# A Mamba-2 mixer whose output is kept channel-major instead of token-major

## The chip, the core and the metric

The kernel runs on one core of a Trainium2 chip. The metric is the time of one execution in microseconds of device time; three runs of the kernel before the change gave 2559.63, 2559.95 and 2562.32 us, so the median is 2559.95 us. Every other time below is from one profiled execution of the same kernel.

The engines' names in the profile are PE (TensorE, products), PEld (TensorE's loading of the stationary operand, which overlaps PE), DVE (VectorE), ACT (ScalarE), POOL (GpSimd) and SP (SyncE, here the queue that starts the weights' DMAs).

## The reference

The model is a decoder trunk for 256 tokens of 2048 channels: a Mamba-2 mixer, a gated feed-forward, an attention layer and another gated feed-forward, each followed by a layer norm. Only the mixer is touched. Cut to what matters:

```
zxbcdt = x @ w_in
z   = zxbcdt[..., :4096]
xbc = silu(causal_dwconv(zxbcdt[..., 4096:10240], conv_w, conv_b))
dt  = softplus(zxbcdt[..., 10240:] + dt_bias)
xs, b, c = xbc split in 4096 channels, 8 groups x 128, 8 groups x 128
a  = -exp(a_log)
y  = ssd_chunked(xs * dt, a * dt, b, c)
y  = y + d_skip * xs
y  = y * silu(z)
yg = y in 8 groups of 512 channels
yg = yg * rsqrt(mean(yg ** 2) + RMS_EPS)
y  = yg * norm_w
return y @ w_out
```

`ssd_chunked` works in two chunks of 128 tokens and in 64 heads of 64 channels (eight heads make a group). With `a_cum` the running sum of `a * dt` inside a chunk, it is

```
decay_in     = exp(a_cum[l] - a_cum[s])            where s <= l, else 0
y_diag[l]    = sum over s of (c[l] . b[s]) * decay_in[l, s] * x[s]
state        = sum over s of b[s] * exp(a_cum[end] - a_cum[s]) * x[s]      (first chunk)
y_off[l]     = exp(a_cum[l]) * (c[l] . state)                              (second chunk)
```

## The kernel before

**Weights and steps.** All weights come as one sequence of 512 KB tiles, one per step. A tile is fetched on SP's queue (`load`, L162), and split into two rounded parts `hi` (ScalarE, L183) and `lo` (VectorE, L184) by `split`; activations are kept as such pairs too, and a product of two pairs is made of three products of parts. `splits` (L188) is called in the middle of a step and makes the split of the step three ahead (`LA = 3`), provided that TensorE has freed the buffer. Sixteen rows of 128 input channels and 512 output channels (a chunk) take eight steps.

**Two modes.** In mode "X" (`half`, L196) a tile of the activations, 128 channels by 128 tokens, is the stationary operand and 512 columns of weights stream past it: twelve products 512 wide in a step, and the result is token-major, 128 tokens on the partitions. In mode "W" (`whole`, L225) a 128x128 tile of weights is the stationary operand and the activations stream: eight products of 512 columns (`hi` with both parts of the activations, L243) and eight of 256 (`lo`, L245) in a step, and the result is channel-major. Odd steps of this mode begin with `lo`, even ones with `hi`. A result of mode "W" lies in PSUM in two halves which `gather` (L545) adds: a copy by ScalarE, then a sum by VectorE.

**The order of the rest.** The order of all instructions is the order in which the program writes them: each engine runs its own list in that order and waits where data are missing. `at(i, f)` (L296) puts a function's instructions behind the products of step i. A group g of the mixer takes sixteen steps from `s0 = chX[g].first`: eight for x (mode "W"), eight for z (mode "X"). Its own work stretches over 30 steps, so the first steps of group g+1 (s0+16 is its first) hold the last work of group g; functions of group g that are put at the same step stand ahead of those of g+1.

**A group's work before the change**, by steps from s0 (L774 to L796):

- s0+3 `m_load`: `a_cum` of eight heads broadcast to all partitions by two DMAs on POOL's queue, tiles A[0] and A[1]. POOL waits for the y_diag of the group before, which reads the same buffers.
- s0+6 `m_cb`: the products of C and B in PSUM (L672, L673), masked by VectorE into `cb`; a copy `bc` of the cross-chunk product by ScalarE (L679).
- s0+6 to s0+8 `m_decay`, `m_exp`: A minus `a_cum` of the token on the partition, capped at 0 (VectorE), then the exponential (ScalarE, with a load of its table). At s0+13 and s0+14 `m_mask` multiplies by `cb`.
- s0+4 to s0+9: gather and four taps of the causal convolution of x (`Conv`, L555; the scaled first tap on ScalarE, L572, three taps on VectorE, L577). s0+12 `x_silu`.
- s0+15 `x_turn`: eight transposes of x to token-major (L707), copied to `xs` by ScalarE. s0+16 `x_dt`: VectorE makes `xdt` (x times dt), `xe` (times the decay to the chunk's end) and x times D in `xs`.
- s0+16 `z_silu`: silu of z out of PSUM.
- s0+18 `y_off` and `y_diag` of the first chunk, s0+19 `y_diag` of the second: for each head a product with A as the stationary tile and 64 columns of `xdt` streaming (L723); the sums go into `xs`.
- s0+21 `z_gate`: times silu(z) on VectorE; squares on ScalarE with their sum over the 512 channels, which lie along the free axis.
- s0+22 `z_rms`: mean plus epsilon (VectorE), power -0.5 (POOL). s0+23 `z_scale`: each token's row times its factor.
- s0+28, s0+29 `z_turn`: four transposes each (L340) back to channel-major, then `norm_w` and the split into the two parts of `yT` (ScalarE, VectorE).

After the last group the chunks of `w_out` read `yT` (mode "X").

Of the kernel before, what the change touches and what calls it, by code (L numbers as in the profile page):

```python
# [24 lines left out]
P = 128  # L25
# [20 lines left out]
for _name, _n in (("cw", 4 * CONV), ("cb", CONV), ("nw", DI), ("fw0", 6 * DFF), ("fcb0", 2 * DFF), ("fw1", 6 * DFF),  # L46
                  ("fcb1", 2 * DFF), ("dtb", P), ("alog", P), ("d", NH * P)):
    COL_AT[_name] = N_COL
    N_COL += _n // P
# [9 lines left out]
def chunks():  # L59
# [14 lines left out]
    for g in range(NG):  # L74
        out += some("W", "mamba_w_in", 0, DI + g * NC, 1, KD) + some("X", "mamba_w_in", 0, z + g * NC, 1, KD)
# [15 lines left out]
def yoco_kernel(ctx: ExitStack, tc: tile.TileContext, x, lmg, lmb, lfg, lfb, x_t, columns, w, out):  # L91
# [449 lines left out]
    d_bc = cols[:, COL_AT["d"]:COL_AT["d"] + NH]  # L541
    acum_d = dram.tile([NH, S], F32, name="acum_d")
    aux = mp.tile([P, 6, NH], F32, name="aux")
# [86 lines left out]
    def dt_cum():  # L630

        u, e, q, r, dt, ac, ex = T["t"]
        nc.vector.tensor_scalar(q, dt, T["an"], None, op0=OP.mult)
        nc.vector.memset(r, 1.0)
        for c in range(2):
            sl = slice(c * P, (c + 1) * P)
            nc.vector.tensor_tensor_scan(ac[:, sl], r[:, sl], q[:, sl], 0.0, op0=OP.mult, op1=OP.add)
        nc.gpsimd.dma_start(acum_d, ac)
        nc.scalar.activation(ex[:, :P], ac[:, :P], AF.Exp, bias=ac[:, P - 1:P], scale=-1.0)
        nc.scalar.activation(ex[:, P:], ac[:, P:], AF.Exp)  # L640

    def dt_turn():
        u, e, q, r, dt, ac, ex = T["t"]
        pt = tp_tile()
        for i, (t, c) in enumerate(((dt, 0), (dt, 1), (ac, 0), (ac, 1), (ex, 0), (ex, 1))):
            nc.tensor.transpose(pt[:, i * NH:(i + 1) * NH], t[:, c * P:(c + 1) * P], ident[:NH, :NH])
        nc.vector.tensor_copy(aux, pt[:, :6 * NH].rearrange("p (a h) -> p a h", h=NH))
# [38 lines left out]

    def m_exp(g, c):
        t = G[g]["A", c]
        nc.scalar.activation(t, t, AF.Exp)
# [12 lines left out]
    def x_turn(g):  # L702
        G[g]["xs"] = xs = t4k("xs")
        for h in range(2):
# [3 lines left out]
            nc.scalar.copy(xs[:, h], ps)  # L708

    def x_dt(g):  # L710
        xs = G[g]["xs"]
        G[g]["xdt"] = xd = t4k("xdt")
        G[g]["xe"] = xe = mp.tile([P, NC], F32, tag="xe", name="xe", bufs=1)
        for h in range(2):
            nc.vector.tensor_mul(heads(xd[:, h]), heads(xs[:, h]), hd(aux[:, h], g))
        nc.vector.tensor_mul(heads(xe), heads(xd[:, 0]), hd(aux[:, 4], g))
        for h in range(2):
            nc.vector.tensor_mul(heads(xs[:, h]), heads(xs[:, h]), hd(d_bc, g))

    def y_diag(g, c):  # L720
        ps = tp_tile()
        for h in range(8):
            nc.tensor.matmul(ps[:, h * 64:(h + 1) * 64], G[g]["A", c][:, h, :],  # L723
                             G[g]["xdt"][:, c, h * 64:(h + 1) * 64], start=True, stop=True)
        y = G[g]["xs"]
        nc.vector.tensor_add(y[:, c], y[:, c], ps)

    def y_off(g):

        ps = tp_tile()  # L730
        nc.tensor.matmul(ps, G[g]["bc"], G[g]["xe"], start=True, stop=True)  # L731
        y, xe = G[g]["xs"], G[g]["xe"]
        nc.vector.tensor_mul(heads(xe), heads(ps), hd(aux[:, 5], g))
        nc.vector.tensor_add(y[:, 1], y[:, 1], xe)

    def z_silu(g):
        G[g]["sz"] = sz = t4k("sz")
        for h in range(2):
            nc.scalar.activation(sz[:, h], chZ[g].part[h], AF.Silu)

    def z_gate(g):
        y, sz = G[g]["xs"], G[g]["sz"]
        nc.vector.tensor_mul(y, y, sz)
        G[g]["ss"] = ss = mp.tile([P, 2, 1], F32, tag="ss", name="ss")
        for h in range(2):
            nc.scalar.activation(sz[:, h], y[:, h], AF.Square, accum_out=ss[:, h, :])

    def z_rms(g):
        G[g]["rr"] = rr = mp.tile([P, 2, 1], F32, tag="rr", name="rr")
        nc.vector.tensor_scalar(rr, G[g]["ss"], 1.0 / NC, RMS_EPS, op0=OP.mult, op1=OP.add)  # L750
        nc.gpsimd.tensor_tensor(rr, rr, mhalf, op=OP.pow)

    def z_scale(g):
        y = G[g]["xs"]
        for h in range(2):
            nc.vector.tensor_scalar(y[:, h], y[:, h], G[g]["rr"][:, h, :], None, op0=OP.mult)

    def z_turn(g, p):
        ps = turn_pair([G[g]["xs"]], p)
        ks = [(4 * g + 2 * p + kk, ps[:, kk * S:(kk + 1) * S]) for kk in range(2)]  # L760
        for k, s in ks:
            nc.scalar.activation(yT[:, k, 0, :], s, AF.Identity, scale=c1("nw", k))
        for k, s in ks:
            nc.vector.scalar_tensor_tensor(yT[:, k, 1, :], s, c1("nw", k), yT[:, k, 0, :].bitcast(F32),
                                           op0=OP.mult, op1=OP.subtract)
# [8 lines left out]
    for g in range(NG):  # L774
        s0 = chX[g].first
        at(s0 + 3, m_load, g)
        at(s0 + 6, m_cb, g)
        at(s0 + 6, m_decay, g, 0)
# [8 lines left out]
        at(s0 + 16, x_dt, g)  # L787
        at(s0 + 16, z_silu, g)
# [310 lines left out]
```

## Time and profile before

| what | value |
|---|---|
| runs | 2559.63, 2559.95, 2562.32 us |
| the profiled execution | 2561.29 us |
| its span on the core | 2559.3 us |
| its mean granted clock of TensorE | 0.998 |
| weights read | 881 DMAs of 512 KB, 3.6 us from issue to landing (median) |
| the decays' DMAs (`m_load`) | 16 of 512 KB, 5.1 us (median) |

The span is what the core's engines show; the profiled execution's own time holds a little more around it. Busy times are sums over one engine; because a product starts before the one ahead of it has left the array, its duration in the profile is longer than its distance to the next.

### The profile page before, as it was taken

The page shows a single profiled execution, that of the slowest core. Times are in us where ns is not written, and L with a number is a line of the kernel's source. Part 1 is how long each engine was busy: PE and PEld are TensorE (multiplying, and loading weights), DVE is VectorE, ACT ScalarE, POOL GpSimd, SP SyncE. Part 2 cuts the span into 40 slices and gives each one's busy share as a digit, 9 for nine tenths or more (in the row PEclk, how much of TensorE's full clock was granted, in tenths as well). Part 3 has the DMA queues.
Part 4 walks back from the last instruction along what each step waited for, and adds up shares of the span by engine and source line. Part 5 has one row for each costly group of instructions (what it writes and reads, how often), then busy time and mean ns, then how long its engine had stood idle before and what let it go on. Part 6 is the DMA issues. An engine that isn't in the chain of part 4 may idle for free.

```text
span 2559.3 us, 35395 instructions
## 1 busy us (share of the span) xinstructions
PE 2544.5 (99%) x13744; PEld 2200.1 (86%) x13744; DVE 1666.9 (65%) x2137; ACT 1299.7 (51%) x1633; POOL 72.2 (3%) x87
## 2 busy tenths in 40 slices
PE   9999999999999999999999999999999999999998
PEld 8888888888888888888888888888888888888887
DVE  6877778754676766666444755655777676765545
ACT  6556556633455555555333444543555555554333
POOL 0000000000100000000000200000200000000001
PEclk9999999999999999999999999999999999999999
DMA  7655555557565555555565655456655555555564
GB/s 248 206 174 191 190 184 180 192 189 231 181 232 188 188 191 190 189 190 189 204 224 198 229 185 175 157 175 222 222 196 185 194 184 194 183 194 201 198 223 164
DMA packets 141495, 500.98 MB, mean 196 GB/s; under 512 B 15616, under 2 KB 16128, under 8 KB 141328
## 3 DMA queue, kind: packets, MB, share of 16 engines
q1 hardware_dynamic: 136976, 483.46, 56.2%
q0 software_dynamic: 4064, 14.75, 1.8%
q8 instruction: 107, 1.75, 0.3%
q14 instruction: 60, 0.49, 0.1%
q10 hardware_dynamic: 288, 0.52, 0.1%
HBM read 490.22 MB, written 8.45 MB: 195 GB/s over the span
## 4 chain that ended last, share of the span: by engine, by line
PE 98%; DVE 1%; issue 0%; ACT 0%; DMA 0%; SPq 0%; DVEq 0%
PE acc L243 36%; PE acc L245 19%; PE acc L211 13%; PE acc L206 13%; PE acc L207 13%; PE tp L723 1%; PE tp L211 0%; PE tp L207 0%; PE tp L206 0%; DVE lo L184 0%; PE tp L340 0%; PE tp L707 0%; PE tp L964 0%; PE tp L731 0%; DVE r L417 0%
## 5 line engine op out<-in xcount | busy, mean ns | idle before, releaser
L184 DVE TENSOR_TENSOR lo<-raw,hi 128x1024 fp32r<-128x1024 f32 (+1 forms) x870 | 1063.6, 1227 | 735.2 <-ACT hi L183 731.3
L183 ACT CAST hi<-raw 128x1024 fp32r<-128x1024 f32 (+1 forms) x870 | 912.5, 1050 | 920.4 <-PE acc L211 378.9
L243 PE MATMUL acc<-hT,hi 128*128 128x512 f32 x3984 | 961.9, 392 | 2.4 <-DVE hT L512 2.4
L243 PEld LDWEIGHTS acc<-hT,hi 128*128 128x128 f32 x3984 | 731.3, 189 | 143.5 <-DVE hT L512 2.6
L245 PEld LDWEIGHTS acc<-hT,lo 128*128 128x128 f32 x3984 | 513.3, 191 | 20.1
L245 PE MATMUL acc<-hT,lo 128*128 128x256 f32 x3984 | 523.4, 283 | 0.0
L207 PE MATMUL acc<-lo,gT 128*128 128x512 f32 (+1 forms) x678 | 254.5, 378 | 0.0
L206 PE MATMUL acc<-hi,gT 128*128 128x512 f32 (+1 forms) x678 | 254.1, 377 | 0.0
L211 PE MATMUL acc<-hi,gT 128*128 128x512 f32 (+1 forms) x678 | 200.8, 377 | 0.0
L206 PE MATMUL acc<-hi,hT 128*128 128x512 f32 x448 | 179.9, 402 | 0.0
L207 PE MATMUL acc<-lo,hT 128*128 128x512 f32 x448 | 175.2, 391 | 0.0
L207 PEld LDWEIGHTS acc<-lo,gT 128*128 128x128 f32 x678 | 127.7, 188 | 23.3
L206 PEld LDWEIGHTS acc<-hi,gT 128*128 128x128 f32 x678 | 127.6, 188 | 23.1
L211 PEld LDWEIGHTS acc<-hi,gT 128*128 128x128 f32 x678 | 124.9, 188 | 23.7
L211 PE MATMUL acc<-hi,hT 128*128 128x512 f32 x448 | 139.3, 392 | 0.6 <-DVE hT L353 0.6
L211 PEld LDWEIGHTS acc<-hi,hT 128*128 128x128 f32 x448 | 83.4, 188 | 20.6 <-DVE hT L353 3.0
L206 PEld LDWEIGHTS acc<-hi,hT 128*128 128x128 f32 x448 | 84.2, 188 | 17.2 <-ACT hT L352 1.3
L206 PE MATMUL acc<-hi,yT 128*128 128x512 f32 (+1 forms) x270 | 98.9, 371 | 0.0
L207 PEld LDWEIGHTS acc<-lo,hT 128*128 128x128 f32 x448 | 84.3, 188 | 16.8 <-DVE lo L184 0.9
L207 PE MATMUL acc<-lo,yT 128*128 128x512 f32 (+1 forms) x270 | 98.6, 369 | 0.0
L211 PE MATMUL acc<-hi,yT 128*128 128x512 f32 (+1 forms) x270 | 77.7, 369 | 0.0
L577 DVE SCALAR_TENSOR_TENSOR g<-u,cols,g 128x254 f32<-128x254 f32 (+1 forms) x176 | 73.5, 477 | 4.8 <-ACT g L572 4.7
(200 smaller groups left out, 1875.8 us busy)
## 6 DMA issues: line engine op xcount, KB each, us to landing
raw<-in_w SPq DMA_DIRECT2D x881, 512.0 KB, 3.6
mA<-acum_d POOLq DMA_DIRECT2D x16, 512.0 KB, 5.1
hres<-r POOLq DMA_DIRECT2D x12, 512.0 KB, 6.2
r<-hres SPq DMA_DIRECT2D x12, 512.0 KB, 5.3
r<-in_x SPq DMA_DIRECT2D x4, 512.0 KB, 5.1
gb<-in_ln_mix_g SPq DMA_DIRECT2D x8, 256.0 KB, 5.4
gb<-in_ln_mix_b SPq DMA_DIRECT2D x8, 256.0 KB, 6.0
gb<-in_ln_ffn_g SPq DMA_DIRECT2D x8, 256.0 KB, 5.0
```

What stands on the lines that cost most here:

```text
L183: nc.scalar.copy(h[:, sl], t[:, sl])
L184: nc.vector.tensor_sub(l[:, sl], t[:, sl], h[:, sl].bitcast(F32))
L206: nc.tensor.matmul(a, th, h[:, kk, sl], start=k == 0, stop=False)
L207: nc.tensor.matmul(a, th, l[:, kk, sl], start=False, stop=False)
L211: nc.tensor.matmul(a, ch.x.lo(k)[:, ts], h[:, kk, sl], start=False, stop=k == ch.nk - 1)
L243: nc.tensor.matmul(banks[j], h[:, kk, js], ch.x.both(k), start=begins, stop=ends, skip_group_check=True)
L245: nc.tensor.matmul(banks[j][:, :S], l[:, kk, js], ch.x.hi(k), start=begins, stop=ends, skip_group_check=True)
L577: nc.vector.scalar_tensor_tensor(d, u[:, i % 2, :S - k], c1(self.at_w, w[n - 1 - k] + self.ia + i), d, op0=OP.mult, op1=OP.add)
L723: nc.tensor.matmul(ps[:, h * 64:(h + 1) * 64], G[g]["A", c][:, h, :], G[g]["xdt"][:, c, h * 64:(h + 1) * 64], start=True, stop=True)
```

## The change

The mixer's output stays channel-major from x to `yT`. x is channel-major after the convolution already, and is transposed only for the operand `xdt`; y is collected in a tile with channels on the partitions. z's chunks change from mode "X" to mode "W", so that z is channel-major too, with a gather in two halves. In `y_diag` operands change places: 64 columns of `xdt` are the stationary tile, the decay tile's 128 columns stream, and even and odd heads are given the left and the right half of the array's columns (`tile_position=(0, 64 * q)`). `y_off` becomes four products, its factor exp(a_cum) is made from A[1] before A[1] is changed (`m_into`). The mean of squares runs over partitions now: a sum of four tiles (`z_sum`), a product with a column of 1/512 (`z_rms`); its inverse root is brought to all partitions by a product of ones with a diagonal matrix (`z_diag`, `z_scale`). `z_turn` goes. Steps are moved: `z_silu` to s0+12 and s0+17, `z_gate` from s0+21 to s0+20, `z_scale` from s0+23 to s0+25.

The order that results around the step where two groups meet, for VectorE and ScalarE, is the order of the calls in the last part of the diff: behind step s0+20 `z_gate`, then the next group's gather; behind s0+21 `z_sum`, then the next group's taps; behind s0+22 `z_rms`, then the next group's `m_cb`, `m_into` and `m_decay`; behind s0+24 `z_diag`, then a gather; behind s0+25 `z_scale`, then taps.

```diff
@@ chunks()
-        out += some("W", "mamba_w_in", 0, DI + g * NC, 1, KD) + some("X", "mamba_w_in", 0, z + g * NC, 1, KD)
+        out += some("W", "mamba_w_in", 0, DI + g * NC, 1, KD) + some("W", "mamba_w_in", 0, z + g * NC, 1, KD)
@@ yoco_kernel()
+    mean = base.tile([P, 1], F32, name="mean")
+    nc.gpsimd.memset(mean, 1.0 / NC)
+    ones = base.tile([P, P], F32, name="ones")
+    nc.gpsimd.memset(ones, 1.0)
...
+    def m_into(g):
+
+        G[g]["eA"] = e = mp.tile([P, 4, P], F32, tag="eA", name="eA", bufs=1)
+        for q in range(2):
+            ps = slice(64 * q, 64 * q + 64)
+            nc.scalar.activation(e[ps], G[g]["A", 1][ps].rearrange("p (j q) l -> p j q l", q=2)[:, :, q, :], AF.Exp)
...
     def x_turn(g):
-        G[g]["xs"] = xs = t4k("xs")
+
+        G[g]["xdt"] = xd = t4k("xdt")
+        G[g]["xe"] = xe = mp.tile([P, NC], F32, tag="xe", name="xe", bufs=1)
         for h in range(2):
             ps = tp_tile()
             for i in range(4):
                 nc.tensor.transpose(ps[:, i * P:(i + 1) * P], G[g]["xc"][:, i, h * P:(h + 1) * P], ident)
-            nc.scalar.copy(xs[:, h], ps)
...
+            nc.vector.tensor_mul(heads(xd[:, h]), heads(ps), hd(aux[:, h], g))
         nc.vector.tensor_mul(heads(xe), heads(xd[:, 0]), hd(aux[:, 4], g))
-        for h in range(2):
-            nc.vector.tensor_mul(heads(xs[:, h]), heads(xs[:, h]), hd(d_bc, g))
+
+    def y_d(g):
+
+        G[g]["y"] = y = t4k("y").rearrange("p a (k t) -> p (a k) t", t=S)
+        for i in range(4):
+            nc.scalar.activation(y[:, i, :], G[g]["xc"][:, i, :], AF.Copy, scale=c1("d", 4 * g + i))
 
     def y_diag(g, c):
+
         ps = tp_tile()
         for h in range(8):
-            nc.tensor.matmul(ps[:, h * 64:(h + 1) * 64], G[g]["A", c][:, h, :],
-                             G[g]["xdt"][:, c, h * 64:(h + 1) * 64], start=True, stop=True)
-        y = G[g]["xs"]
-        nc.vector.tensor_add(y[:, c], y[:, c], ps)
+            j, q = divmod(h, 2)
+            nc.tensor.matmul(ps[64 * q:64 * q + 64, j * P:(j + 1) * P], G[g]["xdt"][:, c, h * 64:(h + 1) * 64],
+                             G[g]["A", c][:, h, :], start=True, stop=True, tile_position=(0, 64 * q))
+        y = G[g]["y"][:, :, c * P:(c + 1) * P]
+        nc.vector.tensor_add(y, y, ps.rearrange("p (j l) -> p j l", l=P))
 
     def y_off(g):
 
         ps = tp_tile()
-        nc.tensor.matmul(ps, G[g]["bc"], G[g]["xe"], start=True, stop=True)
...
+        for j in range(4):
+            nc.tensor.matmul(ps[:, j * P:(j + 1) * P], G[g]["xe"][:, j * P:(j + 1) * P], G[g]["bc"], start=True,
+                             stop=True)
+        e, y = G[g]["eA"], G[g]["y"][:, :, P:]
+        nc.vector.tensor_mul(e, e, ps.rearrange("p (j l) -> p j l", l=P))
+        nc.vector.tensor_add(y, y, e)
+
+    def z_silu(g, half):
+        if half == 0:
+            G[g]["sz"] = t4k("sz").rearrange("p a (k t) -> p (a k) t", t=S)
+        sz = G[g]["sz"][:, 2 * half:2 * half + 2, :]
+        gather(chZ[g], half, sz)
+        nc.scalar.activation(sz, sz, AF.Silu)
+
+    def z_gate(g):
+        y, sz = G[g]["y"], G[g]["sz"]
+        nc.vector.tensor_mul(y, y, sz)
+        nc.scalar.activation(sz, y, AF.Square)
+
+    def z_sum(g):
+        sz = G[g]["sz"]
+        nc.vector.tensor_add(sz[:, :2], sz[:, :2], sz[:, 2:])
+        nc.vector.tensor_add(sz[:, 0], sz[:, 0], sz[:, 1])
+
+    def z_rms(g):
+
+        ps = tp_tile()
...
+            nc.tensor.matmul(ps[:, h:h + 1], G[g]["sz"][:, 0, h * P:(h + 1) * P], mean, start=True, stop=True)
+        rr = mp.tile([P, 2, 1], F32, tag="rr", name="rr")
+        nc.vector.tensor_scalar(rr[:, :, 0], ps[:, :2], RMS_EPS, None, op0=OP.add)
+        nc.gpsimd.tensor_tensor(rr, rr, mhalf, op=OP.pow)
+        G[g]["rr"] = rr
+
+    def z_diag(g):
+        G[g]["rd"] = rd = mp.tile([P, 2, P], F32, tag="rd", name="rd", bufs=1)
...
+            nc.vector.tensor_scalar(rd[:, h], ident, G[g]["rr"][:, h, :], None, op0=OP.mult)
 
     def z_scale(g):
...
-    def z_turn(g, p):
...
+        ps = tp_tile()
+        nc.tensor.matmul(ps[:, :S], ones, G[g]["rd"].rearrange("p h t -> p (h t)"), start=True, stop=True)
+        y = G[g]["y"]
+        for i in range(4):
+            nc.vector.scalar_tensor_tensor(y[:, i, :], y[:, i, :], c1("nw", 4 * g + i), ps[:, :S], op0=OP.mult,
+                                           op1=OP.mult)
+        hi, lo = (yT[:, 4 * g:4 * g + 4, a, :] for a in range(2))
+        nc.scalar.copy(hi, y)
+        nc.vector.tensor_sub(lo, y, hi.bitcast(F32))
@@ for g in range(NG)
         at(s0 + 6, m_cb, g)
+        at(s0 + 6, m_into, g)
         at(s0 + 6, m_decay, g, 0)
...
         at(s0 + 15, x_turn, g)
-        at(s0 + 16, x_dt, g)
-        at(s0 + 16, z_silu, g)
+        at(s0 + 16, y_d, g)
+        for b in range(2):
+            at(chZ[g].ready(b) + b, z_silu, g, b)
         at(s0 + 18, y_off, g)
         at(s0 + 18, y_diag, g, 0)
         at(s0 + 19, y_diag, g, 1)
-        at(s0 + 21, z_gate, g)
+        at(s0 + 20, z_gate, g)
+        at(s0 + 21, z_sum, g)
         at(s0 + 22, z_rms, g)
-        at(s0 + 23, z_scale, g)
-        at(s0 + 28, z_turn, g, 0)
-        at(s0 + 29, z_turn, g, 1)
+        at(s0 + 24, z_diag, g)
+        at(s0 + 25, z_scale, g)
```

More of the change, by code (lines that the diff above doesn't have):

```diff
@@ L540, in yoco_kernel @@
                             channel_multiplier=-1)
[L541 removed]
+    mean = base.tile([P, 1], F32, name="mean")
+    nc.gpsimd.memset(mean, 1.0 / NC)
+    ones = base.tile([P, P], F32, name="ones")
+    nc.gpsimd.memset(ones, 1.0)
     acum_d = dram.tile([NH, S], F32, name="acum_d")
[L543 removed]
+    aux = mp.tile([P, 5, NH], F32, name="aux")
     def gather(ch, half, dst, scale=None):
@@ L741, in z_gate @@
[L741 to L744, printed above, removed]
-        for h in range(2):
[L746 to L751, printed above, removed]
```

31 lines of the change are left out of this document (4 added, 27 removed).

## The prediction

> **What bounds the kernel now.** I read first the page's busy times and its chain of waits.
>
> ```profile
> PE 2544.5 (99%) x13744; PEld 2200.1 (86%) x13744; DVE 1666.9 (65%) x2137; ACT 1299.7 (51%) x1633; POOL 72.2 (3%) x87
> PE 98%; DVE 1%; issue 0%; ACT 0%; DMA 0%; SPq 0%; DVEq 0%
> ```
>
> TensorE is busy 99% of the span and is 98% of the chain. So two things count: what the change adds to or takes from TensorE's own stream, and whether TensorE, which now never waits, will have to.
>
> The change lies in the eight Mamba groups of sixteen steps. The busy times of a stretch as long as one group (us; busy time and count of PE, PEld, DVE, ACT, POOL; granted clock; DMA share; GB/s):
>
> ```profile
> 253.08:304.10 51.02, 51.02 (x281) 43.92 (x281) 40.39 (x56) 29.67 (x41) 2.51 (x3) 1.00 0.57 186
> ```
>
> A group is 51.02 us of unbroken TensorE work; VectorE has 10.6 us to spare and ScalarE 21 us. On average there is room; the order within the group decides.
>
> **TensorE's part.** From the timeline of TensorE (start us, us, engine, line, tiles, shapes, count):
>
> ```profile
> 128.24 0.39 PE L206 MATMUL acc<-hi,hT 128*128 128x512 f32 x1
> 150.01 1.03 PE L707 MATMUL tp<-ident,xc 128*128 128x128 f32 x8
> 261.29 1.02 PE L731 MATMUL tp<-xe,bc 128*128 128x512 f32 x2
> 262.14 1.89 PE L723 MATMUL tp<-xdt,mA 128*128 128x64 f32 x16
> 266.73 1.90 PE L723 MATMUL tp<-xdt,mA 128*128 128x64 f32 x16
> 268.44 2.07 PE L243 MATMUL acc<-hT,hi 128*128 128x512 f32 x8
> 270.34 2.08 PE L245 MATMUL acc<-hT,lo 128*128 128x256 f32 x16
> 272.25 3.82 PE L243 MATMUL acc<-hT,hi 128*128 128x512 f32 x16
> 275.91 1.11 PE L245 MATMUL acc<-hT,lo 128*128 128x256 f32 x8
> 276.86 0.61 PE L672 MATMUL tp<-CT,BT 128*128 128x128 f32 x4
> 277.45 1.20 PE L245 MATMUL acc<-hT,lo 128*128 128x256 f32 x8
> 293.94 0.60 PE L340 MATMUL tp<-ident,xs 128*128 128x128 f32 x4
> 294.29 0.48 PE L206 MATMUL acc<-hi,hT 128*128 128x512 f32 x1
> 294.60 0.40 PE L207 MATMUL acc<-lo,hT 128*128 128x512 f32 x1
> ```
>
> Products overlap at their ends, so I count from start to start.
>
> - z weight-stationary. The old z chunk of the first group, with nothing between its steps, runs from 128.24 to 150.01: 21.77 us. A weight-stationary step has eight products 512 wide (272.25 to 275.91: 3.66 us for sixteen) and eight 256 wide (270.34 to 272.25: 1.91 for sixteen), 2.785 us. Eight are 22.28: **+0.5 us** a group.
> - z_turn goes: four transposes take 0.35 us (293.94 to 294.29), and the first product behind them 0.31 (to 294.60) where a twelfth of an old z step is 0.227; with the next few a little late too I take 0.48 for each of two calls: **-0.96**.
> - z_rms adds two products with a 128-column stationary tile and one moving column. L672 and L673 together, three products with 128 moving columns, take 0.59 us (276.86 to 277.45), 0.2 each. L723's products stream only 64 columns and still cost 1.71 for eight (266.73 to 268.44), 0.214 each. A narrower moving side makes them no cheaper, so two cost **+0.43**; the lower end would be nothing.
> - z_scale adds one product 256 wide in fp32. One 512 wide took 0.85 us (261.29 to 262.14, two records): 0.43, and 0.1 for the break in the stream: **+0.53**.
> - y_off becomes four products 128 wide, 0.79 to 0.86 against 0.85: nothing.
> - y_diag, twice a group, is the open price. No row shows two products in different halves of the array. If they don't overlap, eight cost what L672's kind costs, 1.6 to 1.71 us: no gain. If they overlap fully, four at 0.214: 0.86. Each fp32 product is two records (sixteen for eight products), issued in order, so the second head can begin when the first streams its second record: four pairs of 0.214 and one record more, 0.96. Going into and out of the split array may cost nothing, or each time the tail of a product: 0.39 long, 0.23 from start to start, so 0.16. I take 0.1 and 1.16 in all, **-1.1** a group; the ends are -1.7 and +0.65 (no overlap, four dearest switches).
>
> By the Trainium skill (TensorEngine Tiling (Array Packing), Key Properties) different tiles load and multiply in parallel, but changing the tiling mode drains the engine. No row here shows either. By it alone the call would be 0.86 and two drains.
>
> TensorE's own work: 0.5 - 0.96 + 0.43 + 0.53 - 1.1 = **-0.6 us** a group, -4.8 us over eight; from -9.6 to +9.2.
>
> **The other engines' part.** Removed and added work by itself changes little: VectorE loses the products with D and the scaling by token and gains two gathers, z_sum, z_diag and one wide subtraction, about +2 us of the 10.6 to spare; ScalarE gains four scaled copies for D, the gathers' copies and eA, about +2 of 21. x_turn, with xdt taken straight from PSUM, is ready sooner than today. What happens once (one transpose and one exponential fewer in dt, two small memsets) is nothing beside them. All this hides under TensorE's products; where the cover ends is the walk below. DMA issues stay the same on SP and POOL. But TensorE will have two new waits on VectorE: z_rms needs z_sum, and z_scale's product needs rd. So I walk the queues from the end of the second y_diag (268.44 now, t = 0 below).
>
> ```profile
> 268.66 0.69 DVE L726 TENSOR_TENSOR xs<-xs,tp 128x512 f32<-128x512 f32 x1 [2.77 <-PE tp L723]
> 269.27 1.22 DVE L184 TENSOR_TENSOR lo<-raw,hi 128x1024 fp32r<-128x1024 f32 x1
> 270.40 0.68 DVE L550 TENSOR_TENSOR u<-u,acc 128x512 f32<-128x512 f32 x1
> 272.77 1.22 DVE L743 TENSOR_TENSOR xs<-xs,sz 128x1024 f32<-128x1024 f32 x1
> 275.88 2.55 DVE L577 SCALAR_TENSOR_TENSOR xc<-u,cols,xc 128x255 f32<-128x255 f32 x6 [1.90 <-ACT xc L572]
> 278.35 1.22 DVE L184 TENSOR_TENSOR lo<-raw,hi 128x1024 fp32r<-128x1024 f32 x1
> 279.55 0.42 DVE L675 TENSOR_TENSOR cb<-tp,tri 128x256 f32<-128x256 f32 x1
> 279.89 1.21 DVE L684 TENSOR_TENSOR mA<-mA,aux 128x1024 f32<-128x1024 f32 x1
> 281.13 0.69 DVE L685 TENSOR_SCALAR mA<-mA 128x1024 f32<-128x1024 f32 x1
> 281.74 1.22 DVE L184 TENSOR_TENSOR lo<-raw,hi 128x1024 fp32r<-128x1024 f32 x1
> 282.88 0.88 DVE L756 TENSOR_SCALAR xs<-xs,rr 128x512 f32<-128x512 f32 x2
> 291.67 3.49 DVE L184 TENSOR_TENSOR lo<-raw,hi 128x1024 fp32r<-128x1024 f32 x3
> ```
>
> ```profile
> 267.88 0.58 ACT L549 COPY u<-acc 128x512 f32<-128x512 f32 x1
> 274.02 0.63 ACT L746 ACTIVATE sz<-xs 128x512 f32<-128x512 f32 x1 [2.43 <-DVE xs L743]
> 280.00 0.27 ACT L679 COPY bc<-tp 128x128 f32<-128x128 f32 x1 [2.72 <-DVE cb L675]
> 280.16 1.05 ACT L183 CAST hi<-raw 128x1024 fp32r<-128x1024 f32 x1
> 281.24 1.28 ACT L689 ACT_TABLE_LOAD   x1
> 282.53 1.06 ACT L689 ACTIVATE mA<-mA 128x1024 f32<-128x1024 f32 x1
> ```
>
> Today VectorE has no pause from 275.88 to past 283 and TensorE doesn't feel it: each split is made three steps ahead, and the lo of 281.74 finds its hi (280.16) done, because ScalarE makes it before the exponentials' table load.
>
> After the change, in program order: y's sum at 0.22; lo to 1.96; z_gate, now a step earlier, to 3.1; on ScalarE the square of 1024 (L689's 1.06 for that size) to 4.2, then, behind it, the convolution's copy (0.5) to 4.7 and hi to 5.7. So the gather's sum comes at 4.7, lo at 5.7 to 6.85, z_sum (0.61, 0.34 and 0.1 between) to **7.9**. TensorE wants it after three steps, at 8.4: hidden with half a microsecond over. Taps (2.47) to 10.4, lo to 11.5, cb to 11.95, the first decay (1.85 by 279.89 to 281.74) to 13.8; bc on ScalarE ends at 12.2.
>
> Here m_into stands ahead of the split: table load 1.28 and two exponentials of 64x512 (0.55 each by L746) hold ScalarE to 14.6, and hi ends at 15.6. VectorE, done at 13.8, waits 1.8 us for it, and queued behind are lo (to 16.75), the second decay (18.6), one more lo (19.75) and z_diag: two small operations, below L756's 0.88 for 512 columns, say 0.3, done at **20.05**. TensorE wants rd after six steps (16.7), z_rms and m_cb (1.0) and two breaks (0.1), at **17.8**. It waits **2.2 us**.
>
> What is late next: the gather's sum and a lo take VectorE to 22; z_scale's four operations (0.42 each by L577) to 23.7; ScalarE's copy of 1024 to 24.8; the subtraction to 25.9; the taps to 28.4, and the first of three lo (today at 291.67, with slack) to 29.5. TensorE, free of z_scale's product at 20.6, has run three steps by 28.9, and step s0+29, odd, now begins with lo: **0.7 to 0.9 us** more.
>
> So about 3 us a group, in the seven groups that have a next one: +21 us. Its bounds: half of that, if the new operations are shorter than the rows of their size (10), and 28.
>
> **The sum.** -4.8 + 21 = +16 us. The profiled execution took 2561.3 us with a span of 2559.3, 1.3 us above the median of 2559.95; I put the difference on the median: **2576 us**.
>
> **The rivals.**
>
> 1. The change doesn't do what it says: the two heads don't overlap, only switches are paid. Then TensorE's work is +0.5 to +1.15 a group, 4 to 9 us, with the waits 25 to 30: 2585 to 2590. For it: all L723 shows is that such products are bound by something other than their streaming.
> 2. The clock falls on top. This trace shows it once, at the start (the timeline's row, then three stretches):
>
> ```profile
> 11.01 2.72 PE L243 MATMUL acc<-hT,hi 128*128 128x512 f32 x8 [2.35 <-DVE hT L512]
> 11.01:13.53 2.52, 2.52 (x9) 2.02 (x10) 1.77 (x2) 1.47 (x3) 0.00 (x0) 0.75 1.03 397
> 13.53:15.23 1.70, 1.70 (x9) 1.70 (x8) 0.91 (x2) 1.34 (x2) 0.00 (x0) 0.50 1.05 410
> 15.23:17.30 2.07, 2.07 (x10) 1.67 (x10) 1.18 (x3) 1.28 (x2) 0.00 (x0) 0.89 1.03 408
> ```
>
> After an idle of 2.35 us the granted clock was 0.75 and 0.50, and 1.83 + 0.955 + 1.83 us of work took 6.29: 1.7 us lost. My wait is as long. Seven such falls would add 12: 2588. Against it: there a single start-up, here 50 us of dense work between the waits. [...]
>
> 3. The other side: the cover holds. If ScalarE makes m_into's three instructions about 2 us sooner than my walk has it, so that hi is ready when the first decay ends, z_diag is done before 17.8 and the late lo disappears too. Then TensorE's own balance is the result: -4.8, 2555, or 2550 with full overlap; without overlap 2564. For it: VectorE has slack on average, and the crowd from 275.88 costs TensorE nothing today. Against it: bc already waits for VectorE's cb (2.72 us at 280.00), and the table load has a fixed 1.28. It decides from 2.2 us of relief.
>
> **How the numbers follow.** My forecast, 2568 to 2582, 50%; no overlap 24%; the clock 11%; cover holds 11%, of which 7% is faster and 4% within 0.2%; 4% for worse lag, up to 2600. 0.2%, 5 us, is about what a measurement of this kernel can tell from no change (the runs shown reach from 2559.63 to 2562.32). Range 2563 to 2591. Faster 0.08, same 0.05, slower 0.87.
>
> **What would show it.** A group's length is 53 to 54 us, the granted clock near 1.00. TensorE waits about 2 us for VectorE's rd ahead of the ones product, and for a lo some ten microseconds later; VectorE waits for a hi of ScalarE that stands behind m_into's exponentials. y_diag runs near 1.2 us; at 1.7 the heads don't overlap. It is wrong if TensorE's share stays at 99% with no wait for rd, if the wait lands on z_rms instead, or if the later stages, which nothing touches, change by more than a microsecond.

## The result and the profile after

The changed kernel takes 2599.39 us (median of four runs, 2597.70 to 2600.55) against 2560.77 us before: a ratio of 1.0148, interval 1.0136 to 1.0160. It is slower, as forecast, but by 38.6 us instead of 16. The profiled execution took 2600.55 us with a span of 2598.6 us, 39.3 us more than the span before.

Busy times and chain of waits of the changed kernel's page:

```profile
PE 2564.4 (99%) x14031; PEld 2201.1 (85%) x14031; DVE 1682.4 (65%) x2161; ACT 1317.7 (51%) x1632; POOL 71.6 (3%) x89
PE 90%; DVE 5%; ACT 2%; issue 1%; DMA 0%; SPq 0%; DVEq 0%; ACTq 0%
```

TensorE is 90% of the chain instead of 98%; VectorE and ScalarE hold 7% now. But TensorE's busy time also grew, by 19.9 us, where the sum had it shrink by 4.8. So there are two questions: where TensorE waits, and what made its work longer.

The first: what TensorE waited for (line, what released it: us in all, times, longest), and then the same group as was shown of before (a stretch of one group: length, busy time and count of PE, PEld, DVE, ACT, POOL; granted clock; DMA share; GB/s).

```profile
PE tp L783 <- DVE rd L778: 16.7, 7, 2.4
...
PE acc L245 <- DVE lo L184: 2.1, 4, 0.5
```

```profile
260.35:314.45 54.10, 51.21 (x317) 44.10 (x316) 42.03 (x58) 31.91 (x40) 2.51 (x3) 1.00 0.54 174
```

The two waits of the forecast are there: rd seven times, up to 2.4 us each, and a lo four times, up to 0.5. (The line left out is the start-up's, as before.) The group is 54.10 us long instead of 51.02, at a granted clock of 1.00.

The second question leads to the stages behind the mixer, which the change does not touch. Their time grew from 1861.31 us (687.69 to 2549.00) to 1875.96 (712.44 to 2588.40). Grouped by line and shape, TensorE's products in that stretch (count; busy us, mean ns), first of before, then of after:

```profile
L243 PE MATMUL acc<-hT,hi 128*128 128x512 f32 x3200 | 768.6, 391 | 0.0
L245 PE MATMUL acc<-hT,lo 128*128 128x256 f32 x3200 | 416.5, 283 | 0.0
L206 PE MATMUL acc<-hi,gT 128*128 128x512 f32 x602 | 234.4, 389 | 0.0
```

```profile
L243 PE MATMUL acc<-hT,hi 128*128 128x512 f32 x3200 | 783.4, 396 | 0.0
L245 PE MATMUL acc<-hT,lo 128*128 128x256 f32 x3200 | 413.0, 281 | 0.0
L206 PE MATMUL acc<-hi,gT 128*128 128x512 f32 x602 | 234.4, 389 | 0.0
```

Same lines, same shapes, same counts: what reads hT has another pace (L243 14.8 us slower, L245 3.5 faster), what reads gT has not, to the tenth of a microsecond. In TensorE's timeline of one untouched stretch (start us, us), before and after:

```profile
1004.81 3.82 PE L243 MATMUL acc<-hT,hi 128*128 128x512 f32 x16
1008.46 2.08 PE L245 MATMUL acc<-hT,lo 128*128 128x256 f32 x16
1010.37 3.82 PE L243 MATMUL acc<-hT,hi 128*128 128x512 f32 x16
```

```profile
1004.64 3.89 PE L243 MATMUL acc<-hT,hi 128*128 128x512 f32 x16
1008.37 2.06 PE L245 MATMUL acc<-hT,lo 128*128 128x256 f32 x16
1010.27 3.89 PE L243 MATMUL acc<-hT,hi 128*128 128x512 f32 x16
```

From start to start sixteen 512-wide products take 3.73 us instead of 3.65, sixteen 256-wide ones 1.90 instead of 1.91. No wait stands beside them, and the granted clock over the untouched stages is 1.00 in both; it is a steady pace, for the whole kernel.

By stage, the two profiled executions compare like this (us; the boundaries are the first transposes of x of the first and of the last group, and the first transposes behind the mixer, L348):

| stage | before | after | more |
|---|---|---|---|
| start to the first group's transposes | 150.01 | 152.12 | 2.1 |
| seven groups | 357.14 | 380.78 | 23.6 |
| last group and `w_out` | 180.54 | 179.54 | -1.0 |
| the rest, untouched | 1861.31 | 1875.96 | 14.6 |
| sum | 2549.00 | 2588.40 | 39.4 |

What the change does to the untouched stages can only be indirect. One thing that it changes for the whole program is where tiles lie in SBUF. D is kept by channel now, so `cols` has 32 columns less and everything laid out behind it, hT among it, lies 128 bytes lower on each partition. `mean` and `ones` are new tiles of the `base` pool, and the tiles of the weights (raw, hi, lo), which lie behind that pool, stand 416 bytes higher. So the distance from hT to hi, 54272 bytes before, is 54816 after. That was the first theory: **places**. Its rival was a cause in what is run (a wait or a clock that the trace does not show).

### The profile page after: what moved, and what is told of

Its sections match the earlier page's. It is cut to its first block, busy times and chain, and to the rows that moved or that the text cites. A ratio compares the mean times of both kernels' runs of the same rounds, so it can differ in the third digit from the quotient of the medians.

```text
span 2598.6 us, 36021 instructions
## 1 busy us (share of the span) xinstructions
PE 2564.4 (99%) x14031; PEld 2201.1 (85%) x14031; DVE 1682.4 (65%) x2161; ACT 1317.7 (51%) x1632; POOL 71.6 (3%) x89
## 4 chain that ended last, share of the span: by engine, by line
PE 90%; DVE 5%; ACT 2%; issue 1%; DMA 0%; SPq 0%; DVEq 0%; ACTq 0%
PE acc L243 37%; PE acc L245 19%; PE acc L211 10%; PE acc L207 10%; PE acc L206 10%; DVE lo L184 2%; DVE xc L580 1%; ACT hi L183 1%; PE tp L733 1%; DMA raw<-in_w 0%; PE tp L211 0%; PE tp L207 0%; PE tp L206 0%; ACT L694 0%; DVE y L757 0%
## 5 line engine op out<-in xcount | busy, mean ns | idle before, releaser
L243 PE MATMUL acc<-hT,hi 128*128 128x512 f32 x4496 | 1110.2, 398 | 2.7 <-DVE hT L512 2.5
L243 PEld LDWEIGHTS acc<-hT,hi 128*128 128x128 f32 x4496 | 826.9, 189 | 180.1 <-DVE hT L512 2.7
L245 PEld LDWEIGHTS acc<-hT,lo 128*128 128x128 f32 x4496 | 576.0, 189 | 30.1 <-DVE lo L184 2.8
L245 PE MATMUL acc<-hT,lo 128*128 128x256 f32 x4496 | 586.2, 282 | 2.1 <-DVE lo L184 2.1
L207 PE MATMUL acc<-lo,gT 128*128 128x512 f32 (+1 forms) x678 | 254.5, 378 | 0.0
L206 PE MATMUL acc<-hi,gT 128*128 128x512 f32 (+1 forms) x678 | 254.1, 377 | 0.0
L211 PE MATMUL acc<-hi,gT 128*128 128x512 f32 (+1 forms) x678 | 200.8, 377 | 0.0
L207 PEld LDWEIGHTS acc<-lo,gT 128*128 128x128 f32 x678 | 127.6, 188 | 23.3
L206 PEld LDWEIGHTS acc<-hi,gT 128*128 128x128 f32 x678 | 127.6, 188 | 23.2
L211 PEld LDWEIGHTS acc<-hi,gT 128*128 128x128 f32 x678 | 124.9, 188 | 23.7
L206 PE MATMUL acc<-hi,yT 128*128 128x512 f32 (+1 forms) x270 | 99.0, 371 | 0.0
L207 PE MATMUL acc<-lo,yT 128*128 128x512 f32 (+1 forms) x270 | 98.6, 369 | 0.0
L553 DVE TENSOR_TENSOR u<-u,acc 128x512 f32<-128x512 f32 x108 | 73.5, 681 | 13.7 <-ACT u L552 12.8
L206 PE MATMUL acc<-hi,hT 128*128 128x512 f32 x192 | 79.3, 413 | 0.0
L211 PE MATMUL acc<-hi,yT 128*128 128x512 f32 (+1 forms) x270 | 77.7, 369 | 0.0
L207 PE MATMUL acc<-lo,hT 128*128 128x512 f32 x192 | 76.0, 396 | 0.0
L580 DVE SCALAR_TENSOR_TENSOR v<-u,cols,v 128x254 f32<-128x254 f32 (+1 forms) x176 | 73.1, 477 | 0.0
L941 ACT CAST gT<-v 128x512 fp32r<-128x512 f32 x44 | 27.3, 621 | 84.5 <-DVE v L940 84.5
L552 ACT COPY u<-acc 128x512 f32<-128x512 f32 x108 | 62.2, 577 | 0.0
```

The costliest lines, as they stand in the source:

```text
L206: nc.tensor.matmul(a, th, h[:, kk, sl], start=k == 0, stop=False)
L207: nc.tensor.matmul(a, th, l[:, kk, sl], start=False, stop=False)
L211: nc.tensor.matmul(a, ch.x.lo(k)[:, ts], h[:, kk, sl], start=False, stop=k == ch.nk - 1)
L243: nc.tensor.matmul(banks[j], h[:, kk, js], ch.x.both(k), start=begins, stop=ends, skip_group_check=True)
L245: nc.tensor.matmul(banks[j][:, :S], l[:, kk, js], ch.x.hi(k), start=begins, stop=ends, skip_group_check=True)
L552: nc.scalar.copy(dst, p[:, :, S:])
```

## The experiments

### Are places the cause, and in which kernel?

In the kernel **before**, nothing but tiles is moved: the weights' tiles by 416 bytes, or hT by 128 (D gets a tile of its own, loaded by an extra DMA; a pad keeps the weights' tiles where they were).

```diff
 (b_hilo_moved)
+    base.tile([P, 104], F32, name="pad")
 (b_hT_moved)
-    cols = base.tile([P, N_COL], F32, name="cols")
+    cols = base.tile([P, N_COL - 32], F32, name="cols")
...
-        nc.sync.dma_start(cols, columns)
+        nc.sync.dma_start(cols, columns[:, :N_COL - 32])
+        nc.sync.dma_start(d_bc, columns[:, COL_AT["d"]:])
...
+    base.tile([P, 32], F32, name="pad")
...
-    d_bc = cols[:, COL_AT["d"]:COL_AT["d"] + NH]
+    d_bc = mp.tile([P, NH], F32, name="d_bc")
```

> The kernel before, with 416 bytes a partition put unused ahead of the weights' buffers, so that hi, lo, raw and the later pools lie where the changed kernel has them; hT stays at byte 21216. Question: why does a weight-stationary step (sixteen products 512 wide: 3.655 us before, 3.73 after) cost more in the changed kernel also in stages that the change doesn't touch? Theory H (the place of hT, the streaming operand): 3.655 us, time 2560.8 as before. Rival L (the place of hi and lo): 3.73 us, time about 2574. Rival N (neither; something in the changed program): 3.655 us here and in the next run too.

> The kernel before, with the 64 columns of D in a tile of their own (one small DMA more), so that hT lies at byte 21088 as in the changed kernel, 128 bytes lower; hi, lo, raw stay. Theory H: sixteen products 512 wide take 3.73 us, and 434 weight-stationary steps of before (there are 498, at +0.028 us each) make the time about 2574 to 2575. Rival L and rival N: 3.655 us, 2561.

In the kernel **after**, the old places are restored and nothing else:

```diff
 (a_old_places)
-    cols = base.tile([P, N_COL], F32, name="cols")
+    cols = base.tile([P, N_COL + 32], F32, name="cols")
...
-        nc.sync.dma_start(cols, columns)
+        nc.sync.dma_start(cols[:, :N_COL], columns)
...
-    mean = base.tile([P, 1], F32, name="mean")
+    mean = mp.tile([P, 1], F32, name="mean")
-    ones = base.tile([P, P], F32, name="ones")
+    ones = mp.tile([P, P], F32, name="ones")
```

> The changed kernel with hT, hi, lo, raw and the four-buffer pool at the bytes where the kernel before has them (32 unused columns in cols, the tiles mean and ones in the Mamba pool). Theory H or L: sixteen products take 3.655 us again, and 562 weight-stationary steps at 0.028 us are 15 us: 2599.4 becomes about 2584; the waits for rd (16.7 us) stay. Rival N: 2599.

Measured, against 2560.86 us for before: b_hilo_moved 2588.69 (1.0110, interval 1.0095 to 1.0125), b_hT_moved 2580.42 (1.0077, 1.0062 to 1.0092), a_old_places 2585.56 (1.0097, 1.0081 to 1.0114; 13.8 us under the changed kernel's 2599.39).

Over the whole program, TensorE's groups by line of before and of b_hilo_moved:

```profile
L243 PE MATMUL acc<-hT,hi 128*128 128x512 f32 x3984 | 961.9, 392 | 2.4 <-DVE hT L512 2.4
L206 PE MATMUL acc<-hi,hT 128*128 128x512 f32 x448 | 179.9, 402 | 0.0
```

```profile
L243 PE MATMUL acc<-hT,hi 128*128 128x512 f32 x3984 | 979.9, 396 | 2.3 <-DVE hT L512 2.3
L206 PE MATMUL acc<-hi,hT 128*128 128x512 f32 x448 | 182.2, 407 | 0.0
```

An unused tile of 416 bytes makes the untouched kernel 28 us slower, and its slow products are the same as in the changed kernel: 18.0 us on L243 alone, and 2.3 on L206, where hT and hi have exchanged their parts as stationary and streaming operand; the other two lines of that mode that read hT, L207 and L211, have 2.5 and 2.6 us more. Rival L's 14 us counted mode "W" alone, and 0.028 us a step where half of 3.73 less 3.655 is 0.0375. Moving hT alone costs 20 us. Both moves cost, so neither the place of hT (theory H) nor that of hi and lo (rival L) is the cause by itself. In a_old_places the untouched stretch behind the mixer is back at 1861.29 us, and its timeline has the old pace (41.89 to 45.54: 3.65 us):

```profile
41.89 3.82 PE L243 MATMUL acc<-hT,hi 128*128 128x512 f32 x16
45.54 2.08 PE L245 MATMUL acc<-hT,lo 128*128 128x256 f32 x16
```

So places are shown as the cause of the 14.6 us behind the mixer, in both directions. Nothing that the change computes is in it.

### Which places?

If it is the place of one tile as such, moving both together by 416 bytes must cost as well; if it is the distance between them, it must not. And a distance changed by 512 or 256 bytes tells whether there is a period. A last kernel moves raw, which VectorE and ScalarE read, off its place while hi and lo keep a good distance: that tells whether the operand of the other engines has a part in it.

```diff
 (b_all_moved)
-    cols = base.tile([P, N_COL], F32, name="cols")
+    cols = base.tile([P, N_COL + 104], F32, name="cols")
...
-        nc.sync.dma_start(cols, columns)
+        nc.sync.dma_start(cols[:, :N_COL], columns)
 (b_hilo_512)
+    base.tile([P, 128], F32, name="pad")
 (b_hilo_256)
+    base.tile([P, 64], F32, name="pad")
 (b_raw_off)
+    rawp = ctx.enter_context(tc.tile_pool(name="rawp", bufs=RAW))
+    padp = ctx.enter_context(tc.tile_pool(name="padp", bufs=1))
+    padp.tile([P, 24], F32, name="pad2")
...
-        t = wts.tile([P, 2, NC], F32, tag="raw", name="raw", bufs=RAW)
+        t = rawp.tile([P, 2, NC], F32, tag="raw", name="raw", bufs=RAW)
...
+    base.tile([P, 104], F32, name="pad")
```

> The kernel before, with 416 unused bytes put ahead of hT, so that hT, hi, lo, raw and the later pools all move by 416 bytes and keep their distances (hi lies 54272 bytes above hT, 106 times 512). So far sixteen products 512 wide took 3.655 us at a distance of 54272 (two kernels) and 3.72 to 3.73 at 54400, 54688 and 54816. Theory R (the distance of the two operands decides): 3.655 us and 2561. Rival B (the bytes at which each lies decide, and only 21216 for hT with 75488 for hi is good): 3.72 or more, 2580 or more.

> The kernel before, with 512 unused bytes between hT and the weights' buffers: hi lies 54784 bytes above hT, 107 times 512 and not a multiple of 1024. Theory R with a period of 512 bytes: 3.655 us, 2561. Theory R with a period of 1024 or more: 3.72 us or more, 2575 to 2590. Rival B: as the longer period.

> The kernel before, with 256 unused bytes between hT and the weights' buffers: hi 54528 bytes above hT, a multiple of 256 and not of 512. Distances that are multiples of 512 gave 3.655 us for sixteen products 512 wide, others 3.72 to 3.73. If the period is 512: 3.72 or more, 2575 to 2590. If it is 256: 3.655, 2560.

> The kernel before, with raw (which DMAs write and ScalarE and VectorE read) moved by 416 bytes against hT, and hi and lo by 512. Theory: it is the distance between TensorE's two operands, hT and hi or lo, that counts: 3.655 us for sixteen, 2560. Rival: the other engines' traffic in raw meets TensorE's reads: 3.72 or more, 2575 or more.

Measured: b_all_moved 2560.64 us (0.9998, interval 0.9988 to 1.0008), b_hilo_512 2560.11 (1.0000, 0.9990 to 1.0010); b_hilo_256 2561.58 and b_raw_off 2563.27 (one run each, beside 2560.36 for before; b_raw_off starts later, with 3.4 us of wait for the first hT instead of 2.4).

With all runs together, the distance from hT to hi and what sixteen 512-wide products take from start to start:

| kernel | distance in bytes | rest by 256 | us for sixteen |
|---|---|---|---|
| before, a_old_places, b_all_moved, a_best | 54272 | 0 | 3.65 |
| b_hilo_256 | 54528 | 0 | 3.65 |
| b_hilo_512, b_raw_off | 54784 | 0 | 3.65 |
| b_hT_moved | 54400 | 128 | 3.72 |
| b_hilo_moved | 54688 | 160 | 3.73 |
| after | 54816 | 32 | 3.73 |

For example b_hilo_256, and b_hilo_moved (40.78 to 44.51):

```profile
41.91 3.82 PE L243 MATMUL acc<-hT,hi 128*128 128x512 f32 x16
45.57 2.08 PE L245 MATMUL acc<-hT,lo 128*128 128x256 f32 x16
```

```profile
40.78 3.89 PE L243 MATMUL acc<-hT,hi 128*128 128x512 f32 x16
44.51 2.08 PE L245 MATMUL acc<-hT,lo 128*128 128x256 f32 x16
```

The distance decides, not the place: 0, 256 and 512 bytes more are equally good, while the three distances tried that are no multiple of 256 make these products 2% slower. In b_raw_off, with raw moved by 416 bytes, the pace is the good one. It fits that the products of gT kept theirs: gT lies in a pool that is opened behind the weights' tiles, so in b_hilo_moved it moves with them and keeps its distance to hi. Why the distance matters inside the chip no run shows. lo was always moved with hi, so the two were not told apart.

### What makes rd late?

The forecast blamed `m_into`, which stands ahead of a weights' split in ScalarE's order. If that is wrong, and `z_diag` comes late by VectorE's own load, moving `m_into` cannot help. In a_into_early `m_into` goes one step forward, behind the convolution's work of s0+5; in a_scale_later only the product that needs rd goes one step back.

```diff
 (a_into_early)
-        at(s0 + 6, m_into, g)
...
+        at(s0 + 5, m_into, g)
 (a_scale_later)
-        at(s0 + 25, z_scale, g)
+        at(s0 + 26, z_scale, g)
```

> The changed kernel with m_into moved from s0+6 to s0+5, behind the next group's taps, into the 4.3 us in which ScalarE now waits for cb. My theory (ScalarE's table load and two exponentials ahead of the split delay VectorE and with it rd): VectorE's wait of 2.1 us for hi ahead of the second decay goes, TensorE's wait for rd falls from 2.4 to under 0.5 us in each of seven groups, 2599.4 becomes 2584 to 2588. Rival (VectorE is simply too full there, z_sum and z_diag are the cause): the wait for rd stays above 1.5 us, 2594 or more. Rival (the new place waits for the DMA of A[1]): a wait of ScalarE on that DMA of a microsecond or more shows.

> The changed kernel with z_scale at s0+26 alone (m_into stays at s0+6, places as in the changed kernel). rd is ready 20.5 us after the second y_diag, TensorE asks for it one step (2.8 us) later than now, at 20.7: its wait for rd goes, 16.7 us of waits and the clock's falls with it. If that is all, 2578 to 2583. Rival: the lag of 2 us that m_into brings stays on VectorE, whose lo of the next steps and z_sum come late instead, so that TensorE waits there: 2585 to 2592.

Measured: a_into_early 2582.69 us (1.0085, interval 1.0070 to 1.0100), a_scale_later 2583.23 (1.0090, 1.0061 to 1.0119), so 16.7 and 16.2 us under the changed kernel, both at its places. The first is a little under the range of its theory, the second at the upper end.

The changed kernel's VectorE and ScalarE around the wait (timeline; in brackets the idle time before and what ended it):

```profile
288.73 0.69 DVE L687 TENSOR_SCALAR mA<-mA 128x1024 f32<-128x1024 f32 x1
291.54 1.22 DVE L184 TENSOR_TENSOR lo<-raw,hi 128x1024 fp32r<-128x1024 f32 x1 [2.12 <-ACT hi L183]
295.68 0.47 DVE L778 TENSOR_SCALAR rd<-ident,rr 128x128 f32<-128x128 f32 x2
```

```profile
287.60 0.27 ACT L681 COPY bc<-tp 128x128 f32<-128x128 f32 x1 [4.31 <-DVE cb L677]
287.87 1.28 ACT L694 ACT_TABLE_LOAD   x1
289.17 1.27 ACT L694 ACTIVATE eA<-mA 64x512 f32<-64x512 f32 x2
290.46 1.05 ACT L183 CAST hi<-raw 128x1024 fp32r<-128x1024 f32 x1
```

And a_into_early at the same place of its group: VectorE, then TensorE.

```profile
284.58 0.69 DVE L687 TENSOR_SCALAR mA<-mA 128x1024 f32<-128x1024 f32 x1
285.19 1.22 DVE L184 TENSOR_TENSOR lo<-raw,hi 128x1024 fp32r<-128x1024 f32 x1
289.32 0.48 DVE L778 TENSOR_SCALAR rd<-ident,rr 128x128 f32<-128x128 f32 x2
```

```profile
289.95 0.67 PE L783 MATMUL tp<-rd,ones 128*128 128x256 f32 x2 [0.27 <-DVE rd L778]
```

With m_into out of the way VectorE's 2.12 us of idle are gone, and TensorE's wait falls from 2.38 to 0.27 us: the stall is m_into's, passed on by hi and lo. The wait on a late lo stays (3.6 us in seven groups). In a_scale_later TensorE's products no longer wait for rd or for the late lo of L245; what they still wait for is short:

```profile
PE tp L769 <- DVE sz L763: 1.5, 6, 0.3
PE acc L243 <- ACT hi L183: 1.2, 6, 0.2
```

Its first group takes 50.98 us, the others 52.13 to 52.17: without the long wait TensorE is early enough to meet the next shortages, z_sum and a hi. A third one stands only in the list of the weight loads (PEld): a lo of L245 behind the transposes, 1.7 us in six waits. A wait costs more than its row names: z_rms starts 1.36 us behind the row ahead of it (225.07 to 226.43) in a group where it waits 0.25, and 0.95 (173.74 to 174.69) in the first, where it does not: 0.41 for 0.25. The row counts from the end of the product ahead, and the last 0.16 us of that product (its row is 1.11 long where the next start otherwise comes after 0.95) are covered by the next one only when there is no wait.

### Do the two heads overlap?

The changed kernel gives neighbouring heads to different halves of the array. In a_heads_apart the four even heads come first, then the four odd ones, so that each product follows one in its own half:

```diff
-        for h in range(8):
+        for h in (0, 2, 4, 6, 1, 3, 5, 7):
```

> The changed kernel with y_diag's eight products in another order: the four even heads (left half of the array) first, then the four odd ones (right half), so that neighbours are in the same half. If the 1.02 us that y_diag takes now comes from heads in different halves overlapping, it becomes about 1.7 us (the next product may overlap only once), TensorE's own work grows by 1.4 us a group and the time by 8 to 11 us to 2607 to 2611. Rival (a 64-column stationary tile is simply cheaper to load, nothing overlaps): 1.02 us stays, 2599.

Measured: 2608.06 us (1.0185, interval 1.0167 to 1.0204). TensorE's rows of one call in the changed kernel, then in a_heads_apart:

```profile
270.65 1.09 PE L733 MATMUL tp<-mA,xdt 128*64 128x128 f32 x16
271.67 1.21 PE L245 MATMUL acc<-hT,lo 128*128 128x256 f32 x8
```

```profile
272.91 1.58 PE L733 MATMUL tp<-mA,xdt 128*64 128x128 f32 x16
274.42 1.22 PE L245 MATMUL acc<-hT,lo 128*128 128x256 f32 x8
```

1.02 us for eight heads side by side, 1.51 apart: only the order differs, so neighbours in different halves do overlap. Which part of their work overlaps (loading or streaming) no run shows. Apart, they take less than the expected 1.7; whether that is the one change of half in the middle or a cheaper 64-column tile, no run shows. Two calls in eight groups make 7.8 us, of the 8.7 measured.

### A version from the findings

a_best has the old places, m_into at s0+5 and z_scale at s0+26: the diffs of a_old_places, a_into_early and a_scale_later together.

> The changed kernel with hT, hi, lo and raw at the places of before, m_into at s0+5 and z_scale one step later (s0+26), so that its product waits for nothing and the late lo comes ahead of it. If waits and places are all that the change lost, what is left is TensorE's own balance of -0.2 to -0.8 us a group: a group takes 50.3 to 50.8 us, no wait of TensorE for rd or lo, and 2555 to 2560 us against 2560.9 of before. Rival (a further loss is hidden in the changed kernel): over 2563.

Measured: **2554.88 us** against 2560.54 (0.9979, interval 0.9970 to 0.9988): 0.2% faster than the kernel before, and 1.7% faster than the changed one. Its list of TensorE's waits has no line of a group any more, and the same group as above:

```profile
249.55:299.87 50.32, 50.32 (x318) 44.24 (x317) 42.05 (x59) 31.59 (x41) 2.52 (x3) 1.00 0.57 189
```

TensorE's work without a wait, 50.32 us against 51.02: this is the change's own balance.

## Why the prediction was right in kind and short in size

**The step that failed** is the one that the sum did not hold: that the later stages, which nothing touches, stay as they are. The forecast put them at nothing, and named a change of them by more than a microsecond as a sign that it is wrong. They grew by 14.6 us, and the experiments show why: the change shifts tiles in SBUF, and the distance from hT to hi is no longer a multiple of 256 bytes. 562 steps of mode "W" (4496 products of L243, eight a step) at 0.029 us each ((3.73 - 3.655 + 1.895 - 1.912) / 2, means over many steps) are 16.3 us over the program; with the few steps of mode "X" that read hT (2 us) that is about 18. In the time it is 13.8 us (2599.39 less 2585.56), since in the groups the waits hide a part, and the clock falls more often at the old places. Without it, the sum was nearer: at the old places the changed kernel takes 2585.6 us against the 2576 forecast, inside its range.

**TensorE's own balance** was forecast at -0.6 us a group, -4.8 in all. Measured -0.70 a group, and -5.7 us between a_best and before. Term by term, start to start in the trace of a_best and in that of before (us a group):

| term | forecast | measured | from |
|---|---|---|---|
| y_diag, two calls | -1.1 | -1.37 | 1.03 and 1.02 instead of 1.71 each (1.16 was taken) |
| products beside these calls | | +0.14 | 2.98 between the calls (260.80 to 263.78) instead of 2.88 (263.85 to 266.73); 8.46 behind the second (264.80 to 273.26) instead of 8.42 (268.44 to 276.86) |
| y_off | 0 | +0.13 | 0.98 (258.79 to 259.77) instead of 0.85 |
| z_rms | +0.43 | +0.45 | 0.37 (273.26 to 273.63), and 0.08 more for the products of C and B behind it (0.67 instead of 0.59) |
| z_scale's product | +0.53 | +0.43 | 0.24, and 0.19 more for the eight products behind it (rows below; eight take 0.95 otherwise) |
| z's mode, and z_turn | -0.46 | -0.48 | from the eight products of L243 ahead of z to the next transposes 24.53 (275.34 to 299.87), less the 0.43, instead of 24.58 (278.49 to 303.07) |
| sum | -0.6 | -0.70 | |

```profile
285.51 0.59 PE L783 MATMUL tp<-rd,ones 128*128 128x256 f32 x2
285.75 1.30 PE L245 MATMUL acc<-hT,lo 128*128 128x256 f32 x8
286.89 3.36 PE L243 MATMUL acc<-hT,hi 128*128 128x512 f32 x14
```

Rival 1, no overlap, is refuted by a_heads_apart. The Trainium skill (TensorEngine Tiling (Array Packing), Key Properties) has tiles work in parallel, and the trace agrees; the drain that it has for a change of mode must be small, since a call takes 1.02 us and 0.07 beside it, where four pairs alone, at 0.214, are 0.86 (an estimate: 0.214 is the price of a 128-column tile).

**The waits** came where the walk had them. Times from the end of the second y_diag (275.69), forecast and measured: z_sum done at 7.9 and 7.98 (283.24 and 0.43 later), with z_rms not waiting; VectorE's wait for hi 1.8 and 2.12 us; rd done at 20.05 and 20.46; TensorE's wait for it 2.2 and 2.38; the late lo 0.7 to 0.9 and 0.51, in the groups where the clock did not fall. The rows of TensorE:

```profile
291.89 2.03 PE L243 MATMUL acc<-hT,hi 128*128 128x512 f32 x8
296.30 0.67 PE L783 MATMUL tp<-rd,ones 128*128 128x256 f32 x2 [2.38 <-DVE rd L778]
296.62 2.21 PE L243 MATMUL acc<-hT,hi 128*128 128x512 f32 x8
...
304.30 1.11 PE L245 MATMUL acc<-hT,lo 128*128 128x256 f32 x8
305.91 1.21 PE L245 MATMUL acc<-hT,lo 128*128 128x256 f32 x8 [0.51 <-DVE lo L184]
```

From start to start the first wait costs 2.55 us (4.41 where eight products take 1.865) and the second 0.66 (1.61 instead of 0.95), and the ones product takes 0.32 instead of 0.24: 3.3 us a group in the place of 3.0. That agrees with the groups: 54.10 less 0.46 for the places (sixteen steps) less 50.32 is 3.3. At the old places it is 3.6 (53.94, from 150.80 to 204.74, in the group with no fall of the clock): TensorE arrives sooner and waits longer, so in these groups the wait hides most of what the places cost. Seven groups: 25 us where the sum had 21.

**The clock** (rival 2) fell, but only in some groups, and cheaply. One of the changed kernel's falls, in TensorE's timeline and as a stretch, and the same place of another group, where it did not fall (296.30 above):

```profile
350.40 1.19 PE L783 MATMUL tp<-rd,ones 128*128 128x256 f32 x2 [2.38 <-DVE rd L778]
351.03 3.47 PE L243 MATMUL acc<-hT,hi 128*128 128x512 f32 x8
```

```profile
350.40:354.00 3.60, 3.60 (x9) 2.89 (x10) 3.34 (x6) 0.90 (x1) 0.00 (x0) 0.53 0.60 178
296.00:300.00 4.00, 3.70 (x22) 3.32 (x23) 3.61 (x7) 1.20 (x2) 0.00 (x0) 1.00 0.54 151
```

The same wait of 2.38 us is followed by 0.53 of the clock once, and by 1.00 the other time. It fell in three groups of the changed kernel and in six of a_old_places. Where it fell, eight products took 3.47 us instead of 2.21, but TensorE then came late enough to find lo ready, and the group was only about 0.7 us longer: 2 us in all in the changed kernel, 4 at the old places, where the rival had 12. By the Trainium skill (TensorE: Matmul & The Clock Gate, Part 1) windows of about 3.4 us that run freely decide, and the clock falls after an idle one; that the same wait trips it in some groups alone agrees with free windows, but a wait shorter than a window was enough here.

**The sum again**, for the seven groups of the changed kernel: -0.7 x 7 for TensorE's work, 3.3 x 7 for the waits, 0.46 x 7 for the places and 2 for the clock are +23.4; the stages table has +23.6. Then 14.6 behind the mixer, 2.1 before the first group and -1.0 in the last. Rival 3, that the cover holds, is what a_best is: it forecast 2555 us where ScalarE gets m_into done earlier, and 2554.88 was measured. But the forecast had it decide from 2.2 us of relief for m_into alone; a_into_early shows that this removes the long wait and leaves the lo, and the group is still 52.00 us; in a_best z_scale's later step, and the old places, came with it. What m_into's move does at the old places without that step was not run.

## What to carry to other kernels

A change also moves every tile that is laid out behind the ones it adds or shortens; when stages that it does not touch change their pace, compare the mean of one product there first, and restore the old places before judging the change. A short function put on an engine's queue ahead of a cast that others wait for can cost nearly its whole length at the engine that waits last, however much slack its own engine has on average: here, moving 2.6 us of ScalarE's work away took 2.1 off TensorE's wait of 2.4. Products that use different halves of the array's columns are worth placing next to each other: here 0.49 us for eight.

## What the hardware showed that was not expected

- Sixteen products of hT with hi took 3.65 us when the distance between the two tiles in SBUF was a multiple of 256 bytes (three distances), and 3.72 to 3.73 at the three other distances tried, at a granted clock near 1.00 with no wait shown. In the kernel before, the two such moves cost 20 and 28 us of 2560. Products of the weights with gT, which in b_hilo_moved keeps its distance to hi, kept their 389 ns.
- Eight products of 128x64 stationary tiles take 1.02 us when neighbours use different halves of the columns, 1.51 when they use the same half.
- A wait of TensorE costs about 0.16 us more, from start to start, than its row names (0.41 for 0.25, 0.66 for 0.51, 2.55 for 2.38): the tail of the product ahead is not covered then.
- A wait of 2.4 to 2.5 us in an otherwise dense stream lowered the granted clock, to 0.53 to 0.60 over the 3.6 us behind it, in three of seven groups of the changed kernel and in six of seven at the old places, and not in the others.
